# Bias copies, their source rows and the softmax statistics on GpSimd's DMA queue, with a smaller descriptor scratch

## The chip, the cores and the metric

One core of one Trainium2 chip runs the whole program. The metric is device time of one launch in microseconds (us); less is better. PE is TensorE, DVE VectorE, ACT ScalarE, POOL GpSimd and SP SyncE. SP computes nothing here: it only issues transfers. Every engine works through its own list of instructions in a fixed order, and a waiting instruction holds back all that stands behind it on its engine.

## The reference

Two layers (DEPTH) over 512 tokens of width 1024, batch 1. Each layer norms the residual, projects it once, and feeds four attention branches:

```python
for l in range(DEPTH):
    xn = rms_norm(x, norm_gain[l])
    (A: q k v z iq ik iw), (B: q k v z), (C: q kv pe z), (D: q k v z), gates = combined_projection(xn, w_in[l])
    ya = dsa_attention(...)                  # A: each query keeps its 128 best keys; bias per head and distance
    yb = dilated_mixture(qbm, kbm, b_v, rel_bias)   # B: 3 groups, steps 1, 4, 16
    yc = causal_dense_attention(qc, kc, v)   # C: latent attention with a rotary key
    yd = banded_attention(qd, kd, d_v, D_WINDOW - 1, band_bias(bias_d, 1), sinks[l])   # D
    merged = sum(sigmoid(gates[n]) * ((ys[n] * silu(zs[n])) @ w_branch[l, n]) for n in range(4))
    x = x + merged @ w_out[l]
```

Three things in it matter here. The bias of a score depends only on the distance of query and key: `rel_bias[t5_bucket(distance)]`, a row of numbers per head, shifted by one for each next query. The table `rel_bias` is one for both layers. And B joins its three groups by weights from the softmax maximum and denominator of each:

```python
m_all = jnp.stack(ms)
w = jnp.stack(dens) * jnp.exp(m_all - jnp.max(m_all, axis=0, keepdims=True))
w = w / jnp.sum(w, axis=0, keepdims=True)
return sum(w[g][..., None] * outs[g] for g in range(3))
```

## The kernel before

Products are taken exactly enough in three passes over weights split into a high and a low part: banks of 128 tokens x 384 columns (lines 512 to 514) or of 128 features x 512 tokens (lines 536 to 538). The weights come as a stream of slots. For each slot `next_slot` (397) issues one load on SP (402, tile `cbuf<-wall` in the trace) into a ring of four buffers; ACT makes the high part (405), DVE, and now and then POOL, the low part (411), into a ring of six. A load waits until the buffer that it overwrites has been read.

`plan` gives the order of a layer's jobs: the indexer, branch D (two slots groups, d0 and d1), the input of C, branch C, branch B (four pairs of heads, each with its groups 0, 1, 2 and then a `mix`), branch A, the merges, the output. A scheduler then reorders the instructions of each engine by a simulated timeline, and gives tiles their place in on-chip memory by itself, up to the memory's end.

The bias takes four steps. A one-hot product (335) makes the row of every head, in four chunks of 480 columns; DVE copies a chunk to a tile `th` (337) and a transfer writes it to `gdram` in HBM (338). `make_skew` (340) then has a transfer copy two rows, 128 times each, from HBM to HBM (347; one row for C, whose bias is a mask). There are 21 such copies: 4 for D, 1 for C, 12 for B, 4 for A, all in layer 1; both layers load from them. `load_bias` (365) last loads a tile from a copy with a row pitch one less than the copy's width, so that row i comes out shifted by i (372). `next_skew` takes copies from a list in the order D, C, B, A and puts them behind the weights requested so far by `tc.issue_after`, which orders instructions on SP.

After D's projections, POOL scales the normed queries and keys (660, 776), computes the norms (378, 379, 792, 793), starts the transfers that swap halves of a key tile (701, 702, `U<-U`) and later multiplies probabilities by one over their sum (958), before they are transposed for the product with V.

In B's groups 1 and 2 the tokens stand in another order (by residue class). Their statistics tile `st` therefore goes to HBM (`sd`, 1183) and comes back in token order (`nat`, 1185); the second transfer waits until the first has landed. The `mix` starts with `mn` on DVE (1111, 1112), which waits for `nat`.

Of the kernel before, what the change touches and what calls it, by code (L numbers as in the profile page):

```python
# [22 lines left out]
NT = S // 128  # L23
# [59 lines left out]
def job_slots(job):  # L83
    """Per weight slot: a list of (source, rows of 128, columns)."""
    kind = job[0]
    if kind in ("idx", "cin", "pair", "d0", "d1"):
        c = chunk_cols(job)
        return [[("w_in", 2 * i + j, c) for j in range(2)] for i in range(4)]
    if kind == "z":
        c = Z_OFF[job[1]] + job[2] * 128 + np.arange(128)  # L90
        return [[("w_in", 4 * i + j, c) for j in range(4)] for i in range(2)]
    if kind == "merge":
        n, ft = job[1], job[2]
        c = OFF_G + n * D + ft * 128 + np.arange(128)
        f = ft * 128 + np.arange(128)
        return [[("w_in", j, c) for j in range(6)],
                [("w_in", j, c) for j in (6, 7)] + [(("w_branch", n), j, f) for j in range(4)]]
    if kind == "out":
        f = job[1] * 128 + np.arange(128)
        return [[("w_out", 4 * i + j, f) for j in range(4)] for i in range(2)]  # L100
    if kind == "cq":
        q = job[1] * 384 + np.arange(384)
        return [[("w_q_b", 0, q), ("w_q_b", 1, q)]]
    if kind == "ckv":
        p = job[1]
        h = np.arange(64)
        kv = np.concatenate([(2 * p) * 128 + h, (2 * p + 1) * 128 + h,
                             (2 * p) * 128 + 64 + h, (2 * p + 1) * 128 + 64 + h])
        return [[("w_kv_b", 0, kv)]]
    raise ValueError(kind)  # L110


def plan():
    """The order of a layer's work; what comes first is preferred where several pieces are ready."""
    w = [("idx",)]
# [126 lines left out]
def build(ctx, tc, A, depth=2, dump=None):  # L242
# [46 lines left out]

# [1 line left out]
    def m_tiles():  # L291
# [26 lines left out]
    def later_consts():  # L318
        sy.dma_start(rope, A["rope"])
        sf = T([128, 512], F32, "ssq")[:, :384][:38].rearrange("p (g c) -> p g c", g=3)  # L320
        sy.dma_start(sf, A["sel"])
        ve.tensor_copy(sel, sf)
        rb = T([128, 256], F32, "qn")[:33, :C_ROW + 1]
        sy.dma_start(rb, A["relb"])
        rhl = T([128, 1024], F32R, "qk")[:33, :2 * (C_ROW + 1)].rearrange("p (e c) -> p e c", e=2)
        ve.tensor_copy(rhl[:, 0], rb)
        ve.tensor_tensor(rhl[:, 1], rb, rhl[:, 0], op=OP.subtract)
        for i in range(4):
            oh = T([128, 512], F32, "tmp")[:33, :480]
            sy.dma_start(oh, A["onehot"][:, i * 480:(i + 1) * 480])  # L330
            ohr = T([128, 1024], F32R, "qk")[:33, :480]
            ac.copy(ohr, oh)
            o = ps_t()
            for e in range(2):
                mm(o[:C_ROW + 1, :480], rhl[:, e], ohr, start=e == 0, stop=e == 1)
            gs = T([128, 512], F32, "th")[:C_ROW + 1, :480]
            ve.tensor_copy(gs, o[:C_ROW + 1, :480])
            sy.dma_start(gdram[:, i * 480:(i + 1) * 480], gs)

    def make_skew(seg, r):  # L340
        """Rows r and r + 1 of a segment, 128 copies each, so that a load can shift copy i by i."""
        r0, nr = (C_ROW, 1) if seg == "C" else (SEG_ROWS[seg][0] + r, 2)
# [3 lines left out]
        g = gdram[r0:r0 + nr, o:o + w]  # L346
        sy.dma_start(d, bass.AP(tensor=g.tensor, offset=g.offset, ap=[[SEG_LEN, nr], [0, 128], [1, w]]))
        for i in range(nr):
# [10 lines left out]
    def next_skew():  # L359
        """The next segment's copies, behind the weights requested so far."""  # L360
        if skews:
# [3 lines left out]
    def load_bias(row, seg, n):  # L365
        """[128, n] tile whose row i is the segment's row shifted by i to the right."""
        while (seg, row) not in skew:
# [7 lines left out]
    def rsqrt(eng, r, ss, n, scale, eps=EPS):  # L375
        """r = 1 / sqrt(ss * scale + eps) on [128, n]."""
        y = T([128, 8], F32, "nx")[:, :n]
# [4 lines left out]
    def layer(l, xt):  # L382
# [1 line left out]
        lay = cbuf[:, 520:1440]  # L384
# [7 lines left out]
        sy.dma_start(pk, A["pk"][l][:, :PK])  # L392
# [1 line left out]
        wpos, lcnt = [0], [0.0]  # L394
# [18 lines left out]

# [1 line left out]
        def gain_parts():  # L415
            """x * gain as hi and lo per row tile: the first products need not wait for the norm."""
            xg = [T([128, 2, 512], F32R, "y") for _ in range(4)]
# [56 lines left out]

# [1 line left out]
        pn = ps_t()  # L476
# [40 lines left out]
        def t_banks(slots, w, x):  # L517
            """Banks of all token tiles, filled together; x: hi and lo per row tile."""
            os = [ps_acc() for _ in range(NT)]
# [11 lines left out]
        def f_bank(parts, mh, ml, w=S):  # L531
            """parts: (hi, lo) stationary views [128, 128] per row tile; moving operands mh, ml: [128, w] each."""
            o = ps_acc()
# [10 lines left out]
        def split_ps(hi, lo, src, scale=None):  # L544
            """hi + lo = src (* scale), src in PSUM."""
            if scale is None:
# [10 lines left out]

# [1 line left out]
        def do_idx():  # L559
# [76 lines left out]

# [1 line left out]
        def evac(o, n, scale=1.0):  # L638
            """A copy of a bank's first n columns, so that the bank is free before the norms are known."""
            raw = T([128, 512], F32, "raw")[:, :n]  # L640
# [6 lines left out]
        def norm_qk(o, t, x, gi, scale=1.0):  # L647
            """o: two heads of q and of k in PSUM; hi and lo of the normed ones to x[:, t], [128, 4, 2, 64]."""
            o = evac(o, 256, scale)
# [19 lines left out]
        def q_out(uq, qx, hf, h0, n, perm):  # L669
            """Heads of qx [128, 2, n, 2, 64] (half hf of the tokens) to uq[:, h0:h0 + n], feature-major."""  # L670
            for i0 in range(0, n, 2):
# [12 lines left out]
        def k_out(kk, x, hf, perm):  # L684
            """The two k heads of x (half hf of the tokens), hi on top of lo, to kk(h, 0)."""
            p = ps_t(F32R)
# [11 lines left out]
        def k_swap(kk):  # L698
            """kk(h, 1): lo on top of hi."""
            for h in range(2):  # L700
# [82 lines left out]
        def do_cin():  # L783
# [21 lines left out]
            for i, c in enumerate((R_CQ, R_CQS)):  # L805
                ve.tensor_tensor(rtab[:, i], rope[:, i], pk[:, None, c:c + 32].to_broadcast([128, NT, 32]), op=OP.mult)
            # rotary key, shared by the heads
            t1 = T([128, 256], F32, "qn")[:, :128][:, :NT * 32].rearrange("p (t d) -> p t d", t=NT)
# [23 lines left out]
        def do_cq(p, cT):  # L832
            """The normed and rotated queries of two pairs, [128, 2, 4, 96] per half of the tokens."""
            h, lo = next_slot(("cq", p))
# [64 lines left out]

# [1 line left out]
        STEPS = {  # L901
# [5 lines left out]
        def scores(kind, step, qk, bias, nm, den, mask, sink, both):  # L907
            """exp of the scores less their maximum, sums to den, minus the maximum to nm."""
            s = ps_s()
# [51 lines left out]
        def attend(kind, qk, v, bias, nm, den, norm, both, mask=None, sink=None):  # L961
            """qk(qb, k0, n): (lhsT, rhs) of the passes; v(kb): stationary [128, 128]; nm/den [128, NT] columns.
            Returns the O bank: rows of V's high part on top of rows of its low part."""
            o = ph = pl = None
# [72 lines left out]
        def o_sum(dst, o, h, perm):  # L1037
            """Add the halves of an O bank into rows h*64.. of dst, in token order."""
            a, b = (0, 64) if h == 0 else (64, 0)
# [102 lines left out]

# [1 line left out]
        ys = [[None] * 4 for _ in range(4)]  # L1144
# [3 lines left out]
        for w in PLAN:  # L1148
# [20 lines left out]
            elif kind == "attB":  # L1169
# [11 lines left out]
                if g:  # L1181
                    sd = T([128, 16], F32, "sd", dp)
                    sy.dma_start(sd, stt_[:, g].rearrange("p t a h -> p (t a h)"))
                    sv = sd.rearrange("p (t e) -> (p t) e", e=4).rearrange("(t j) e -> j t e", j=128)
                    sy.dma_start(nat[:, g].rearrange("p t a h -> p t (a h)"), sv)
            elif kind == "mix":
# [142 lines left out]
```

## Time and profile before

| | us |
|---|---|
| median of 3 runs | 1953.87 (1952.23 to 1957.49) |
| profiled execution, span | 1949.2 |
| PE busy in it | 1884.5 (97%) |
| DVE busy | 1331.1 (68%) |
| ACT busy | 1103.0 (57%) |
| POOL busy | 728.5 (37%) |

For the profiled execution no time of its own is given beside its span; the median of the runs is 4.7 us above the span. Matmuls are pipelined, so PE's 97% says that PE rarely stands, not that it does its work at the highest rate: the granted clock has to be looked at as well, and where PE does stand it is asked what ended the wait. Waits of the other engines cost nothing unless PE waits for them in turn. A letter q behind an engine's name (SPq, POOLq) is its instruction queue, where transfers are issued.

### The profile page before, as it was taken

How to read it: one execution, taken by the hardware profiler on the slowest of the kernel's cores; microseconds unless marked ns; L12 is line 12 of the kernel's file. 1: busy time of each engine (PE TensorE's matmuls, PEld its weight loads, DVE VectorE, ACT ScalarE, POOL GpSimd, SP SyncE). 2: the span in 40 equal slices, each digit the busy share in tenths (PEclk: the TensorE clock that was granted, in tenths of full speed). 3: DMA queues.
4: the chain of work that ended last, by engine and by line, in shares of the span. 5: the costliest groups of instructions: out<-in, count | busy, mean ns of one | idle time of the engine just before them, and what ended most of it. 6: DMA issues, size and time to landing. Idle time of an engine off the chain costs nothing.

```text
span 1949.2 us, 33221 instructions
## 1 busy us (share of the span) xinstructions
PE 1884.5 (97%) x11348; PEld 1695.6 (87%) x11348; DVE 1331.1 (68%) x3410; ACT 1103.0 (57%) x2650; POOL 728.5 (37%) x1186
## 2 busy tenths in 40 slices
PE   8759999999989999999999999999999999999999
PEld 7648889989878998998889988899899989898887
DVE  7649777758476866665469888676768686766542
ACT  6538666656455565554347776566555656555431
POOL 3615353424233346640005345253343343755000
PEclk9879999999989999999999999999999999999999
DMA  4223233342334243332252222233333333333233
GB/s 163 84 91 95 67 90 103 105 113 88 110 105 118 80 121 105 99 98 82 91 187 85 82 66 93 74 88 83 94 105 113 101 101 91 117 96 101 80 92 108
DMA packets 103420, 193.47 MB, mean 99 GB/s; under 512 B 21510, under 2 KB 35924, under 8 KB 103252
## 3 DMA queue, kind: packets, MB, share of 16 engines
q1 hardware_dynamic: 92372, 173.52, 29.4%
q0 software_dynamic: 10880, 17.83, 4.2%
q8 instruction: 90, 1.47, 0.3%
q14 instruction: 78, 0.64, 0.1%
HBM read 168.84 MB, written 12.83 MB: 93 GB/s over the span
## 4 chain that ended last, share of the span: by engine, by line
PE 88%; DMA 4%; DVE 2%; ACT 2%; POOL 2%; issue 1%; SPq 1%; DVEq 0%; ACTq 0%; POOLq 0%
PE acc L537 14%; PE acc L536 14%; PE acc L538 14%; PE acc L512 9%; PE acc L513 9%; PE acc L514 9%; PE S L923 4%; PE T L994 3%; PE T L1014 2%; DMA cbuf<-wall 1%; DMA sd<-st 1%; PE T L1033 1%; PE T L1026 1%; PE T L676 1%; PE T L689 1%
## 5 line engine op out<-in xcount | busy, mean ns | idle before, releaser
L411 DVE TENSOR_TENSOR cbufr<-cbuf,cbufr 128x768 fp32r<-128x768 f32 (+3 forms) x396 | 357.6, 906 | 140.5 <-ACT cbufr L405 139.0
L405 ACT CAST cbufr<-cbuf 128x768 fp32r<-128x768 f32 (+3 forms) x396 | 304.9, 774 | 262.4 <-PE acc L537 195.9
L513 PE MATMUL acc<-cbufr 128*128 128x384 f32 (+1 forms) x1152 | 365.8, 318 | 0.0
L512 PE MATMUL acc<-cbufr 128*128 128x384 f32 (+1 forms) x1152 | 364.1, 317 | 0.0
L514 PE MATMUL acc<-cbufr 128*128 128x384 f32 (+1 forms) x1152 | 363.9, 316 | 0.0
L536 PE MATMUL acc<-cbufr 128*128 128x512 f32 x896 | 354.5, 396 | 0.9 <-ACT raw L642 0.9
L538 PE MATMUL acc<-cbufr 128*128 128x512 f32 x896 | 353.9, 395 | 0.0
L537 PE MATMUL acc<-cbufr 128*128 128x512 f32 x896 | 353.6, 395 | 0.0
L513 PEld LDWEIGHTS acc<-cbufr 128*128 128x128 f32 x1152 | 218.7, 190 | 3.0 <-issue 1.1
L512 PEld LDWEIGHTS acc<-cbufr 128*128 128x128 f32 x1152 | 218.5, 190 | 2.7 <-ACT U L696 0.7
L514 PEld LDWEIGHTS acc<-cbufr 128*128 128x128 f32 x1152 | 218.7, 190 | 2.3 <-issue 0.8
L379 POOL TENSOR_TENSOR nr<-nx,cbuf 128x4 f32<-128x4 f32 (+2 forms) x200 | 211.6, 1060 | 11.1
L538 PEld LDWEIGHTS acc<-cbufr 128*128 128x128 f32 x896 | 168.9, 188 | 34.0
L536 PEld LDWEIGHTS acc<-cbufr 128*128 128x128 f32 x896 | 169.0, 189 | 32.7 <-ACT raw L642 1.3
L537 PEld LDWEIGHTS acc<-cbufr 128*128 128x128 f32 x896 | 169.1, 189 | 32.3 <-issue 0.7
L958 POOL TENSOR_SCALAR P<-P,rd 128x128 f32<-128x128 f32 x192 | 117.3, 621 | 195.4 <-DVE rd L956 136.2
L378 POOL TENSOR_SCALAR nx<-nss 128x4 f32<-128x4 f32 (+2 forms) x200 | 62.3, 311 | 272.2 <-DVE nss L653 243.1
L701 POOL DMA_DIRECT2D U<-U x68 | 39.3, 578 | 311.4 <-ACT U L693 190.4
L547 ACT CAST PT<-T 128x128 fp32r<-128x128 f32 (+2 forms) x224 | 102.9, 478 | 64.0 <-PE T L994 38.0
L548 DVE TENSOR_TENSOR PT<-T,PT 128x128 fp32r<-128x128 f32 (+2 forms) x224 | 119.8, 548 | 22.0 <-ACT PT L547 20.3
L945 ACT ACTIVATE P<-P,nm 128x128 f32<-128x128 f32 x192 | 101.9, 533 | 57.4 <-DVE nm L942 56.7
L642 ACT COPY raw<-acc 128x256 f32<-128x256 f32 (+2 forms) x192 | 70.4, 377 | 107.9 <-PE acc L514 74.9
(256 smaller groups left out, 3954.0 us busy)
## 6 DMA issues: line engine op xcount, KB each, us to landing
cbuf<-wall SPq DMA_DIRECT2D x284, 384.0 KB
cbuf<-wall SPq DMA_DIRECT2D x96, 256.0 KB
U<-U POOLq DMA_DIRECT2D x136, 128.0 KB, 2.8
bias<-skew SPq DMA_DIRECT2D x32, 128.0 KB
bias<-skew SPq DMA_DIRECT2D x16, 256.0 KB
skew<-gdram SPq DMA_DIRECT2D x8, 384.0 KB
cbuf<-wall SPq DMA_DIRECT2D x8, 328.0 KB
skew<-gdram SPq DMA_DIRECT2D x4, 640.0 KB
```

The lines of the kernel that those rows point to most:

```text
L379: gp.tensor_tensor(r, y, mhalf[:, :n], op=OP.pow)
L405: pin(ac.copy(h, raw))
L411: pin(e.tensor_tensor(lo, raw, h, op=OP.subtract))
L512: mm(o[:, :c1 - c0], x[kt][:, 0, ts], h[:, a + c0:a + c1], start=kt == 0, stop=False)
L513: mm(o[:, :c1 - c0], x[kt][:, 0, ts], lo[:, a + c0:a + c1], start=False, stop=False)
L514: mm(o[:, :c1 - c0], x[kt][:, 1, ts], h[:, a + c0:a + c1], start=False, stop=kt == KT - 1)
L536: mm(o[:, :w], h, mh[kt], start=kt == 0, stop=False)
L537: mm(o[:, :w], h, ml[kt], start=False, stop=False)
L538: mm(o[:, :w], lo, mh[kt], start=False, stop=kt == n - 1)
L547: ac.copy(hi, src)
L548: ve.tensor_tensor(lo, src, hi, op=OP.subtract)
L958: gp.tensor_scalar(p[:, off:off + nk * 128], p[:, off:off + nk * 128], rd[:, qb:qb + 1], 0.0, op0=OP.mult, op1=OP.add)
```

## The change

Four calls move from SP (`sy`) to GpSimd (`gp`): the write of the bias rows (338), the copies (347), the statistics' way out (1183) and their way back (1185). The loads of weights (402) and of shifted bias tiles (372) stay on SP. The scratch in which descriptors of GpSimd's transfers are kept becomes 4096 bytes per partition instead of the default 16384; tiles may then lie in the 12 KB that become free. All else in the diff is comments.

```diff
@@ later_consts
             ve.tensor_copy(gs, o[:C_ROW + 1, :480])
-            sy.dma_start(gdram[:, i * 480:(i + 1) * 480], gs)
+            gp.dma_start(gdram[:, i * 480:(i + 1) * 480], gs)
@@ make_skew
         g = gdram[r0:r0 + nr, o:o + w]
-        sy.dma_start(d, bass.AP(tensor=g.tensor, offset=g.offset, ap=[[SEG_LEN, nr], [0, 128], [1, w]]))
+        gp.dma_start(d, bass.AP(tensor=g.tensor, offset=g.offset, ap=[[SEG_LEN, nr], [0, 128], [1, w]]))
@@ layer, attention of B
                     sd = T([128, 16], F32, "sd", dp)
-                    sy.dma_start(sd, stt_[:, g].rearrange("p t a h -> p (t a h)"))
+                    gp.dma_start(sd, stt_[:, g].rearrange("p t a h -> p (t a h)"))
                     sv = sd.rearrange("p (t e) -> (p t) e", e=4).rearrange("(t j) e -> j t e", j=128)
-                    sy.dma_start(nat[:, g].rearrange("p t a h -> p t (a h)"), sv)
+                    gp.dma_start(nat[:, g].rearrange("p t a h -> p t (a h)"), sv)
@@ module
-    nc = bacc.Bacc("TRN2", target_bir_lowering=False, num_devices=1)
+    nc = bacc.Bacc("TRN2", target_bir_lowering=False, num_devices=1, dynamic_dma_scratch_size=4096)
```

SP's list, from the last one-hot loads in layer 1 on, before: `gdram<-th` are the four chunks, `skew...` and `skewC` the copies.

```order
L330 DMA tmp_590<-onehot 33x480
L402 DMA cbuf<-wall 128x512
L338 DMA gdram<-th_567 41x480
L338 DMA gdram<-th_577 41x480
L347 DMA skewC_1298<-gdram 128x1x640
L402 DMA cbuf<-wall 128x512
L338 DMA gdram<-th_587 41x480
L402 DMA cbuf<-wall 128x512
L347 DMA skew_0_600<-gdram 256x1x384
L338 DMA gdram<-th_597 41x480
L347 DMA skew_2_602<-gdram 256x1x384
L347 DMA skew_4_1051<-gdram 256x1x384
```

The same place on SP now:

```order
L330 DMA tmp_590<-onehot 33x480
L402 DMA cbuf<-wall 128x512 x4
L372 DMA bias_1301<-skew_0_600 128x256
L372 DMA bias_1366<-skew_0_600 128x256
L372 DMA bias_1473<-skew_2_602 128x256
L402 DMA cbuf<-wall 128x512 x2
L402 DMA cbuf<-wall 128x768
```

Between two of SP's weight loads there is now nothing but loads of bias tiles. On POOL in the same stretch, now (`qk` is the tile of normed queries and keys, `U` a key tile):

```order
L338 DMA gdram<-th_567 41x480
L338 DMA gdram<-th_577 41x480
L378 TENSOR_SCALAR nx_971<-nss_968 128x6
L616 AFFINE_SELECT cbuf<-cbuf 128x128
L379 TENSOR_TENSOR nr_970<-nx_971,cbuf 128x6
L347 DMA skewC_1298<-gdram 128x1x640
L347 DMA skew_0_6521<-gdram 256x1x640
L347 DMA skew_2_6827<-gdram 256x1x640
L347 DMA skew_4_7172<-gdram 256x1x640
L347 DMA skew_6_7583<-gdram 256x1x640
L660 TENSOR_SCALAR qk_608<-qn_644 128x4x64
```

The four copies for A, the largest and the last to be used, come ahead of those for D, since the chunks that they read are written first. Further down POOL's list, ahead of the first multiplication of D's probabilities, now:

```order
L347 DMA skew_2_4372<-gdram 256x1x256
L701 DMA U_142_605<-U_142_605 64x512
L702 DMA U_142_605<-U_142_605 64x512
...
L347 DMA skew_4_4717<-gdram 256x1x384
L347 DMA skew_4_5127<-gdram 256x1x256
L347 DMA skew_4_5269<-gdram 256x1x256
L347 DMA skew_6_5623<-gdram 256x1x384
L347 DMA skew_6_5968<-gdram 256x1x256
L347 DMA skew_6_6379<-gdram 256x1x256
L379 TENSOR_TENSOR nr_1141<-nx_1142,cbuf 128x2
...
L958 TENSOR_SCALAR P_1310<-P_1310,rd_1318 128x128
```

All 21 copies now stand on POOL ahead of D's attention, where before eight stood on SP up to there and thirteen later, between the weights of C and B. A transfer of GpSimd waits in addition, by the semaphores that it is given in turn, until the transfer eight before it on GpSimd has landed. In B the two transfers of the statistics follow one another on POOL:

```order
L660 TENSOR_SCALAR qk_4579<-qn_4658 128x4x64
L1183 DMA sd_4460<-st_3976 128x16
L1185 DMA nat_3977<-sd_4460 128x4x4
L701 DMA U_1056_4476<-U_1056_4476 64x512
```

Before, SP had a load of weights between the two; now POOL itself waits between them until `sd` has landed, and the swap of the next key tile stands behind. In all, SP has 361 rows in its list before and 282 now, POOL 1175 and 1232.

## Rows read from the trace of the kernel before

**Rows 1.** Waits of PE in the whole span: total, times, longest us.
```profile
PE T L803 <- DVE PT L796: 22.3, 1, 22.3
PE T L1026 <- DVE PT L548: 12.3, 3, 5.2
PE T L676 <- ACT raw L642: 11.7, 1, 11.7
```

**Rows 2.** Chain of waits, 60 to 140 us: start, us, what.
```profile
81.64 14.50 DMA gdram<-th
...
113.80 7.30 SPq L347
...
121.62 13.52 DMA cbuf<-wall
```

**Rows 3.** Busy time by stretch: PE, PEld, DVE, ACT, POOL, PEclk, DMA share, GB/s.
```profile
86.00:96.00 10.00, 0.00 (x0) 0.00 (x0) 0.00 (x0) 0.00 (x0) 0.00 (x0) 0.57 0.13 50
...
122.00:135.00 13.00, 0.00 (x0) 0.00 (x0) 0.00 (x0) 0.00 (x0) 0.00 (x0) 0.50 0.25 85
```

**Rows 4.** Waits of all engines, 40 to 200 us.
```profile
POOL P L958 <- DVE rd L956: 34.3, 6, 26.6
...
ACT raw L642 <- DMA gdram<-th: 15.4, 1, 15.4
```

**Rows 5.** Lines 478, 1015 us apart: count, ns min/median/max, first and last start.
```profile
L478 PE MATMUL T<-cbuf,s x8: 251/251/272, 25.1 to 25.9; 128*128 128x2 f32 x8
...
L478 PE MATMUL T<-cbuf,s x8: 167/251/251, 1015.6 to 1016.3; 128*128 128x2 f32 x8
```

**Rows 6.** Chain of waits, first C heads and first two mixes of each layer.
```profile
199.69 0.77 PE T L895 x7
...
437.11 0.89 PE S L1135 x3
...
554.16 0.89 PE S L1135 x3
...
1154.73 0.77 PE T L895 x7
...
1388.72 0.89 PE S L1135 x3
...
1488.52 0.89 PE S L1135 x3
```

**Rows 7.** Chain of waits, 376 to 545 us, statistics of layer 1.
```profile
384.24 7.49 DMA sd<-st
...
528.75 10.47 DMA sd<-st
```

**Rows 8.** Waits of SP's queue, whole span; then SP's timeline in layer 2.
```profile
SPq L1185 <- DMA sd<-st: 46.5, 16, 9.8
...
1338.70 0.33 SPq L1183 DMA_DIRECT2D sd<-st  x1
...
1341.65 0.38 SPq L1185 DMA_DIRECT2D nat<-sd  x1
```

**Rows 9.** Lines 347 and 701: ns min/median/max, first and last start.
```profile
L347 SPq DMA_DIRECT2D skew<-gdram x20: 587/595/9925, 80.9 to 571.6; - x20
...
L701 POOL DMA_DIRECT2D U<-U x68: 514/584/754, 80.6 to 1799.3; - x68
```

**Rows 10.** Transfers of the whole span: line's tiles, times issued, KB of each.
```profile
skew<-gdram SPq DMA_DIRECT2D x8, 384.0 KB
...
skew<-gdram SPq DMA_DIRECT2D x4, 640.0 KB
skew<-gdram SPq DMA_DIRECT2D x8, 256.0 KB
```

**Rows 11.** POOL's timeline, 62 to 145 us and 376 to 402 us.
```profile
142.77 0.83 POOL L958 TENSOR_SCALAR P<-P,rd 128x128 f32<-128x128 f32 x2 [26.60 <-DVE rd L956]
...
399.88 0.63 POOL L701 DMA_DIRECT2D U<-U  x1 [19.74 <-ACT U L693]
```

## The prediction

> **What bounds the kernel now.** I read the waits of PE first, since PE is busy for 97% of the span and only its own idle time, or a lower rate, can be given back. Three waits carry nearly all of it: 22.3 us at line 803, 11.7 us at line 676, and 12.3 us in three pieces at line 1026 [rows 1]. The named releasers (DVE, ACT) are short instructions, so I asked what these had waited for. In the chain of waits between 60 and 140 us stand transfers and SP's queue: the last chunk of bias rows takes 14.50 us to land, SP stands 7.30 us in a copy of line 347, and then a weight slot takes 13.52 us [rows 2]. ACT waits 15.4 us for that chunk before it may write `raw`, which is what PE wants at line 676 [rows 4]. POOL waits 26.6 us just then, for DVE, so it is not the late one [rows 4, 11].
>
> What makes them late is seen in the busy time by stretch. From 86 to 96 us no engine computes anything, and the DMA share is 0.13, 50 GB/s: two engines of sixteen (2/16 = 0.125) [rows 3]. Only a copy is in flight there. A copy has two rows on its slowest dimension, and a 384 KB copy at 50 GB/s takes some 7.7 us; SP's 7.30 us in one is the same time. So before the change the copies go one behind the other on the same two engines, and SP waits with them; a weight slot or chunk, which needs all of its parts, waits behind them too. From 122 to 135 us PE is idle again, with a weight under way [rows 2, 3]. These idle stretches also have a granted clock of 0.57 and 0.50, near or at the 1.2 GHz level in place of 2.4 GHz.
>
> How much could come back is measured by layer 2, which does the same work without copies. From line 478 to the first C heads (line 895) layer 1 takes 199.69 - 25.1 = 174.6 us, layer 2 1154.73 - 1015.6 = 139.1 us [rows 5, 6]: 35.5 us. Of these 22.3 + 11.7 = 34.0 us are PE's two waits; the rest I leave to the bias product, which layer 1 alone has. From line 895 to the second mix layer 1 takes 354.5 us and layer 2 333.8 us [rows 6]: 20.7 us, of which 17.3 lie between the first and the second mix (117.1 against 99.8). There `sd` takes 7.49 and 10.47 us to land, against 1341.65 - 1338.70 = 2.9 us in layer 2 [rows 7, 8], and PE has its 12.3 us at line 1026. The copies run on until 571.6 us [rows 9]: thirteen of 21 come late, among B's weights. After the second mix both layers keep the same pace, so about 35 + 21 = 56 us is all that there is.
>
> **The change part by part.** *Copies leave SP.* Weights no longer stand behind copies in SP's queue. The wait at line 803 (22.3 us) goes whole: the slot of 13.52 us would land as others do. Of line 676's 11.7 us I leave 5: its chunk now follows five copies on POOL's queue, and if those are spread over other engines, it shares some with them for a part of the 14.50 us it takes today.
>
> *Copies come to POOL.* 21 copies and 4 chunks are 25 issues at about 0.58 us, the price of POOL's own transfers [rows 9]: 14.5 us. Between 70 and 115 us POOL is itself needed for scaling and norms; it also has gaps, 26.6 us of waiting before the first line 958 [rows 4, 11]. I take half as exposed, 7.5 us (bounds: 0 if the gaps take all of it, 14.5 if none). Behind the copies stand the swaps of `U` and the norms of C's input, and PE's scores and C's projections wait for these. That is the price if POOL only issues. If it must stand while a copy runs, as SP does, the price is another (first rival).
>
> *The thirteen late copies go early.* In B nothing then holds up `sd` or weights. Of 20.7 us I take 18 back; the rest is work that layer 1 may order differently (bounds 12.3, PE's named waits alone, and 20.7).
>
> *The statistics.* POOL waits between the two transfers for `sd`: 16 times 2.9 us = 46 us of standing, the sum that SP's queue has today (46.5 us [rows 8], with layer 1's slow ones in it). Behind it on POOL stand swaps of key tiles and norms of the next pair. POOL has gaps of the right kind, such as 19.74 us before the swap at 399.88 us [rows 11], and SP no longer stands there. I take 4 us, a quarter of a microsecond for each, between -5 (weights come earlier in B) and +46 (nothing hidden), nearer the low end since that gap is several times the standing.
>
> *Smaller scratch.* 12 KB per partition more for tiles: PE's waits name no buffer, so nothing. A ring a quarter the size may hold fewer descriptors: priced in the rival.
>
> Sum: -(34.0 - 5 - 7.5) - 18 + 4 = -35.5 us. The profiled span of 1949.2 becomes 1913.7, and with the 4.7 us by which the median stands above it, 1918 us. The terms' bounds give 1953.9 - 34.0 - 20.7 - 5 = 1894 at best. With 11.7 left at line 676, 14.5 of issue exposed and 12.3 back in B, the standing as taken, it is 1953.9 - 7.8 - 12.3 + 4 = 1938; the standing's own upper end of 46 would add 42 more and is left to the wide range. I take 1900 to 1938 as this case's own range.
>
> A rule of the Trainium skill speaks against the gain: transfers started by different engines end on the same 16 DMA engines and interleave, and starting from several engines saves only the time of starting them ("DMA: Bandwidth & Descriptors", Issuing engines are not separate DMA queues). In this trace starting is not small, 7.30 us for a copy [rows 2], so the rule and a gain can both hold; taken literally it would leave the copies' 50 GB/s as it is, which is the first rival. Another section of that page (Why a DMA increments its semaphore by 16 and not by 1) says that a GpSimd transfer of few parts takes consecutive engines from a cursor that moves on, where SP's takes the lowest ones always. The two engines of rows 3 fit SP's half; no run here yet shows GpSimd's. By it eight copies in flight would use all 16 engines, and the forecast holds.
>
> **The rivals.** *First: the copies still run one at a time and POOL stands for them.* The 21 copies are 8 x 384 + 4 x 640 + 8 x 256 + 320 = 8000 KB [rows 10], the 320 being that of C in the lists of the change. At 384 KB in 7.3 us that is 152 us. All stand on POOL ahead of the first line 958. They can start at about 72 us, so line 958 would start at about 224 instead of 142.8 us [rows 11]: 81 us late. PE's list holds D's transposes behind that and the early waits are swallowed; the late part still gives 18 back. 1953.9 + 81 - 18 + 4 = 2021 us. For it: the copies' form, two parts, is unchanged; SP stood for copies just so; the scratch is cut to a quarter; the four largest copies, for A, now run first. Against: POOL's transfers so far took 0.51 to 0.75 us each, two or four together, without standing [rows 9]. It decides once about one copy is in flight at a time; at one and a half, the delay is 152/1.5 - 71 = 30 us, and the sum is still slower. Range 1960 to 2060.
>
> *Second: two to three copies in flight, gains and delays nearly cancel.* With two, the copies end at 72 + 76 = 148 us: line 958 is some 5 us late and the early 21.5 us do not come; late part and statistics as above: 1953.9 + 5 - 18 + 4 = 1945. With more POOL standing in B (16 times 1 us in place of a quarter) 1957. So 1936 to 1960. For it: a POOL transfer waits for the landing of the one eight before, so the queue is not free either; and a share of the chunk lands behind copies as today.
>
> *Third: it doesn't do what it says*, because line 803 or B's pace hangs on something else, such as the ring of weight buffers. Against it stands layer 2, which has the same rings and no such waits. It would leave 1950 to 1958, a chance of 0.03.
>
> **How the numbers follow.** The forecast has 0.55, the first rival 0.28, the second 0.14, the third 0.03. This kernel's runs tell 0.3%, about 6 us, from no change. Faster, below 1948: all of the forecast (0.54) and somewhat under half of the second (0.06), 0.60. Within 0.3%, 1948 to 1960: 0.05 of the second, 0.01 of the forecast and 0.02 of the third, 0.08. Slower: 0.28 and 0.04, 0.32. The range for 8 in 10 goes from 1899 to 2020: a tenth is left above it, half of the first rival, and a few hundredths below. Likeliest: 1918 us.
>
> **What would show it.** If right: SP's timeline from 64 to 140 us has no issue of 7 us or more; no stretch with a DMA share of 0.13 and idle engines; PE's waits at lines 803 and 676 are gone or small; a copy's issue on POOL lasts under 1 us; the first line 958 starts at 105 to 125 us; `sd` lands in about 3 us in both layers; the first to the second mix takes about 100 us in layer 1. Layer 2 keeps its pace within a few us. The first rival shows as issues of line 347 of 5 us and more on POOL and a line 958 after 190 us. If line 958 is early and the mixes are late, the statistics' term was mis-sized; if line 803 still waits for a weight, the copies hold the engines and not the queue.

## The result and the profile after

The changed kernel takes 2084.98 us (median of 4 runs, 2083.68 to 2086.16) against 1953.14 us for the kernel before: a ratio of 1.0668, 95% interval 1.0653 to 1.0683, 132 us slower. The forecast was 1918 us, and the range up to 2020 us did not hold the time either. The likeliest case was wrong in sign. The first rival, that GpSimd stands for one copy at a time, is what the trace shows, at a higher price than it was given.

The profiled execution has a span of 2084.4 us, 135.2 us above that of before. First the waits of PE after the change (total, times, longest, in us), to be held against [rows 1]:

```profile
PE T L676 <- DVE qk L777: 80.0, 1, 80.0
PE T L676 <- DVE qk L661: 40.9, 1, 40.9
PE T L803 <- DVE PT L796: 40.1, 1, 40.1
PE S L923 <- DMA U<-U: 9.4, 1, 9.4
```

Four waits make 170.4 us, where 35.3 us stood at the same places before (22.3, 11.7 and, at line 923, 1.3). The wait in B at line 1026 has gone from 12.3 to 1.8 us, so what was hoped for in B did come. DVE, the named releaser, is again only a link: its `qk` at lines 661 and 777 needs the two products of POOL at lines 660 and 776, and its `PT` at line 796 needs POOL's norm `nr` of line 379. DVE's own waits from 60 to 300 us show it:

```profile
DVE PT L796 <- POOL nr L379: 93.0, 2, 48.0
...
DVE qk L777 <- POOL qk L776: 44.7, 3, 37.4
...
DVE qk L661 <- POOL qk L660: 44.1, 1, 44.1
```

POOL's timeline says why its products are late (start, us, engine, line, operation, count, idle time before and what ended it):

```profile
71.88 1.10 POOL L347 DMA_DIRECT2D skew<-gdram  x1
88.72 1.08 POOL L347 DMA_DIRECT2D skew<-gdram  x1 [15.74 <-issue]
104.37 1.05 POOL L347 DMA_DIRECT2D skew<-gdram  x1 [14.57 <-issue]
119.91 1.06 POOL L347 DMA_DIRECT2D skew<-gdram  x1 [14.48 <-issue]
120.99 0.79 POOL L660 TENSOR_SCALAR qk<-qn 128x256 fp32r<-128x256 f32 x2
...
223.90 0.57 POOL L776 TENSOR_SCALAR qk<-qn 128x128 fp32r<-128x128 f32 x2
...
290.73 1.06 POOL L347 DMA_DIRECT2D skew<-gdram  x1 [7.48 <-issue]
291.81 0.72 POOL L379 TENSOR_TENSOR nr<-nx,cbuf 128x2 f32<-128x2 f32 x1
...
293.44 0.83 POOL L958 TENSOR_SCALAR P<-P,rd 128x128 f32<-128x128 f32 x2
```

The first of A's copies goes out at once. Each of the next three waits 14 to 16 us, for no semaphore that the profile shows ("issue"), and the scaling at line 660, which stood at 69.99 us before, starts at 120.99 us. The last copy is issued at 290.73 us, and the first line 958 follows at 293.44 us, against 142.77 us [rows 11]. How long POOL stands, and how long a copy takes, is in line 347's own view and in the page's list of transfers (times issued, KB, us to landing):

```profile
L347 POOL DMA_DIRECT2D skew<-gdram x20: 1054/1063/1154, 71.9 to 290.7; - x20
...
issue: 176.4, 19
```

```profile
skew<-gdram POOLq DMA_DIRECT2D x8, 384.0 KB, 10.7
...
skew<-gdram POOLq DMA_DIRECT2D x4, 640.0 KB, 15.3
skew<-gdram POOLq DMA_DIRECT2D x8, 256.0 KB, 8.4
skewC<-gdram POOLq DMA_DIRECT2D x1, 320.0 KB, 4.4
```

Ahead of the last copy nineteen others of two rows have to land: 8 x 10.7 + 4 x 15.3 + 7 x 8.4 = 205.6 us. From 71.88 to 290.73 us are 218.9, 7.4 of them spent waiting for the last chunk. So these copies go one at a time, the next issued when the one before has landed; only C's, which has one row, goes out beside A's first, at 71.24 us. In between lie long stretches in which no engine computes (POOL's 1.15 us are two issues; busy time by stretch; PE, PEld, DVE, ACT, POOL, granted clock, DMA share, GB/s), and the share of the DMA engines is again that of two of sixteen, as in [rows 3]:

```profile
95.00:120.00 25.00, 0.00 (x0) 0.00 (x0) 0.00 (x0) 0.00 (x0) 1.15 (x2) 0.50 0.13 44
```

The rest of the account comes from the same two markers as in the prediction, line 895 and layer 2's line 478; first before, then after (count, ns, first and last start):

```profile
L895 PE MATMUL T<-cbuf,cq x64: 270/273/279, 197.8 to 1262.0; 128*96 128x128 f32 x64
```

```profile
L895 PE MATMUL T<-cbuf,cq x64: 270/273/280, 348.3 to 1395.6; 128*96 128x128 f32 x64
...
L478 PE MATMUL T<-cbuf,s x8: 167/251/252, 1149.5 to 1150.2; 128*128 128x2 f32 x8
```

Up to line 895 the loss is 348.3 - 197.8 = 150.5 us, which is the delay of line 958 (150.7). From there to layer 2 the stretch shrinks from 1015.6 - 197.8 = 817.8 to 801.2 us: 16.6 us come back. Layer 2 to the end takes 934.9 us against 933.6. 150.5 - 16.6 + 1.3 = 135.2 us.

### The profile page after: what moved, and what is told of

The parts are those of the page before. It is cut to its first block, busy times and chain, and to the rows that moved or that the text cites. A ratio compares the mean times of both kernels' runs of the same rounds, so it can differ in the third digit from the quotient of the medians.

```text
span 2084.4 us, 33192 instructions
## 1 busy us (share of the span) xinstructions
PE 1888.2 (91%) x11348; PEld 1696.3 (81%) x11348; DVE 1334.1 (64%) x3410; ACT 1104.0 (53%) x2650; POOL 757.3 (36%) x1243
## 5 line engine op out<-in xcount | busy, mean ns | idle before, releaser
L958 POOL TENSOR_SCALAR P<-P,rd 128x128 f32<-128x128 f32 x192 | 112.5, 597 | 185.4 <-DVE rd L956 111.5
L676 PE MATMUL T<-cbufr,qk 128*128 128x128 f32 x320 | 44.1, 249 | 120.9 <-DVE qk L777 80.0
L676 PEld LDWEIGHTS T<-cbufr,qk 128*128 128x128 f32 x320 | 35.4, 143 | 123.9 <-DVE qk L777 80.4
## 6 DMA issues: line engine op xcount, KB each, us to landing
skew<-gdram POOLq DMA_DIRECT2D x8, 384.0 KB, 10.7
skew<-gdram POOLq DMA_DIRECT2D x4, 640.0 KB, 15.3
```

The lines of the kernel that those rows point to most:

```text
L958: gp.tensor_scalar(p[:, off:off + nk * 128], p[:, off:off + nk * 128], rd[:, qb:qb + 1], 0.0, op0=OP.mult, op1=OP.add)
```

## The experiments

Theory R says that the descriptor scratch is the limit: a copy gives 128 parts to each of only two DMA engines, and 4096 bytes have room for one such copy. Its rivals are S, that copies of GpSimd's queue are serial by nature, and E, that the two DMA engines are the limit whatever is in flight. All kernels below are cut from the two kernels by a line or two; times are medians, ratios are to the kernel before on the same chip.

**Twice the scratch.**

```diff
-dynamic_dma_scratch_size=4096
+dynamic_dma_scratch_size=8192
```

> The changed kernel with a descriptor scratch of 8192 bytes in place of 4096; nothing else. Theory R (room): the changed kernel's copies go one at a time because each gives 128 parts to each of two DMA engines, and the scratch of 4096 has room for the parts of one copy beside those of small transfers, not of two. With twice the scratch at least two, perhaps three, are in flight: GpSimd's 176 us of standing before line 347 fall to 50 to 90 us, the first line 958 starts at 145 to 185 us instead of 293, and the time is 1940 to 1985 us. Theory S (serial): copies of GpSimd's queue run one behind the other whatever the scratch: the standing stays near 176 us and the time within 10 us of 2085. Theory E (engines): more are in flight, but on the same two DMA engines: GpSimd stands less before the first ones, but all copies together still take some 200 us, and the time stays above 2040.

Measured: 1957.02 us, ratio 1.0021 (1.0011 to 1.0031). 128 us of the 132 are gone with this number alone. POOL's timeline now shows three copies leaving together and the fourth waiting:

```profile
70.20 3.22 POOL L347 DMA_DIRECT2D skew<-gdram  x3
88.24 1.07 POOL L347 DMA_DIRECT2D skew<-gdram  x1 [14.82 <-issue]
...
105.99 3.30 POOL L347 DMA_DIRECT2D skew<-gdram  x3 [7.52 <-DMA gdram<-th]
```

```profile
L347 POOL DMA_DIRECT2D skew<-gdram x20: 1054/1066/1154, 70.2 to 163.6; - x20
...
issue: 50.5, 11
```

The standing falls from 176.4 to 50.5 us and the copies are issued by 163.6 us. S is out. So is E: a 384 KB copy still lands in a median of 12.1 us with up to three in flight, against 10.7 alone, so the copies in flight were not sharing two engines. Even so the kernel is no faster than before, since PE still waits for POOL's products, 10.8 us by way of line 661 and 25.9 by way of line 777:

```profile
PE T L676 <- DVE qk L777: 25.9, 1, 25.9
```

The change with the default scratch of 16384 bytes was not run.

**Half as many parts in each transfer.**

```diff
-        gp.dma_start(d, bass.AP(..., ap=[[SEG_LEN, nr], [0, 128], [1, w]]))
+        for c in (0, 64):
+            gp.dma_start(d[:, c:c + 64], bass.AP(..., ap=[[SEG_LEN, nr], [0, 64], [1, w]]))
```

> The changed kernel with each copy made by two transfers of 64 repeats: same bytes, same scratch, same two engines for each transfer, 64 parts on each instead of 128. Theory R (room): three halves fit where one whole did, one and a half times as much is in flight: 220 us of copying become about 147, the first line 958 starts near 220 us, time 1990 to 2040 us. If one transfer at a time were the rule, whatever its size: 2080 to 2100.

Measured: 1965.80 us (two runs, 1965.29 and 1966.32), ratio 1.0069 (1.0051 to 1.0088); better than expected. Line numbers are one higher in it.

```profile
70.46 2.45 POOL L348 DMA_DIRECT2D skew<-gdram  x3
82.06 0.81 POOL L348 DMA_DIRECT2D skew<-gdram  x1 [9.15 <-issue]
```

With 4096 bytes, three halves leave together and the fourth waits, just as three whole copies did with 8192. That is room counted in parts: 3 x 64 on an engine fit and 4 x 64 don't; 1 x 128 fits and 2 x 128 don't; with 8192, 3 x 128 fit and 4 x 128 don't. It is not counted in bytes moved: at 4096 one copy of 640 KB fits, but two of 256 KB don't; where one follows another in the changed kernel, it waits 7.5 to 7.7 us. The size of the gain was missed because I scaled the 220 us by 1.5; the copies are all issued by 186 us, 116 us after the first, since half of a 384 KB copy lands in 8.1 us and three halves are in flight.

**The same copies over 16 engines, still on GpSimd.**

```diff
-        gp.dma_start(d, bass.AP(..., ap=[[SEG_LEN, nr], [0, 128], [1, w]]))
+        gp.dma_start(d.rearrange("r c w -> c r w"), bass.AP(..., ap=[[0, 128], [SEG_LEN, nr], [1, w]]))
```

> The changed kernel with the 128 repeats as the slowest dimension of a copy instead of the two rows: same bytes, same order, 16 DMA engines instead of two, 16 parts for each. Theories R and E: no standing before line 347 beyond a few us, copies land in 2 to 4 us, first line 958 at 100 to 120 us, time 1905 to 1925 us. Theory S: a shorter copy stands less too, 21 times 3 to 4 us, first line 958 near 150 us, time 1940 to 1955.

Measured: 1923.37 us, ratio 0.9849 (0.9835 to 0.9864). The standing is gone, as R says: with 4096 bytes four of these copies leave together, each of as many parts as before in all, but with 16 on an engine. So it is the parts on one engine that count, not those of the whole copy. The kernel is faster than before, but the first line 958 comes at 127.7 us and not by 120. What is late now (busy time by stretch, then waits between 60 and 150 us, the last of them SP's from 60 to 140):

```profile
100.00:110.00 10.00, 0.51 (x3) 0.08 (x1) 0.00 (x0) 0.00 (x0) 4.84 (x13) 0.64 1.01 286
110.00:120.00 10.00, 5.51 (x14) 4.40 (x15) 5.73 (x17) 3.28 (x6) 5.79 (x9) 0.51 1.00 285
```

```profile
ACT cbufr L405 <- DMA cbuf<-wall: 23.2, 4, 19.3
DVE cbufr L411 <- ACT cbufr L405: 17.8, 3, 17.2
...
PE T L676 <- DVE qk L777: 14.0, 1, 14.0
```

```profile
SPq L372 <- DMA skew<-gdram: 23.8, 2, 23.1
```

ACT waits 19.3 us for a weight slot, DVE for ACT, and PE for the `qk` that stands behind this on DVE. Two things make the weight late. SP stands 23.1 us, until 95.8 us, at the load of a bias tile (line 372) that waits for its copy, and the weights stand behind it. And all 21 copies go out between 70 and 114 us, so that the DMA engines are full: 256 KB loads of weights from 99 to 116 us land in 10.5 us, where the median of the whole run is 2.7. Another queue for the copies spares the weights neither.

**Only the copies back on SP.**

```diff
-        gp.dma_start(d, bass.AP(...))
+        sy.dma_start(d, bass.AP(...))
```

> The changed kernel with line 347 alone back on SP; chunks and statistics stay on GpSimd, scratch 4096. All theories: the loss of 131 us is the copies' alone, so the time is near that of before: 1940 to 1965 us. The first line 958 near 143 us. If the statistics' standing on GpSimd were worth what its upper bound said (46 us), it would be 1985 to 2000.

Measured: 1943.21 us, ratio 0.9950 (0.9935 to 0.9965). The loss is the copies' alone; chunks and statistics on GpSimd gained 10 us beside copies on SP. PE's wait at line 803 stays (28.1 us), that at line 676 goes.

**Only the smaller scratch.**

```diff
-bacc.Bacc("TRN2", target_bir_lowering=False, num_devices=1)
+bacc.Bacc("TRN2", target_bir_lowering=False, num_devices=1, dynamic_dma_scratch_size=4096)
```

> The kernel before with a descriptor scratch of 4096 bytes, nothing else. Theory R: only the swaps U<-U use it, and they are small: same, 1948 to 1959 us. If the smaller scratch by itself cost something (waits of GpSimd before line 701) or gave something through tiles' places, the time would differ by over 6 us and GpSimd's wait before line 701 would have changed.

Measured: 1953.29 us, ratio 0.9998 (0.9989 to 1.0008): nothing. The smaller scratch costs only together with transfers that fill it.

**Only the statistics on GpSimd, beside the kernel before.**

```diff
-                    sy.dma_start(sd, ...)
+                    gp.dma_start(sd, ...)
-                    sy.dma_start(nat[:, g]..., sv)
+                    gp.dma_start(nat[:, g]..., sv)
```

> The kernel before with lines 1183 and 1185 alone on GpSimd; copies and chunks stay on SP, scratch as before. It splits the 10 us that the version with only the copies back on SP was below before. Theory A (the statistics): sd lands in about 3 us, no load of weights stands behind nat's wait on SP, the wait at line 1026 goes from 12.3 to under 6 us, time 1941 to 1948 us. Theory B (the chunks, whose landing fell from 14.5 to 3.5 us, and the wait at line 676): 1950 to 1957 us.

Measured: 1946.82 us, ratio 0.9969 (0.9958 to 0.9980). This is theory A: PE's wait at line 1026 falls from 12.3 to 3.4 us, while line 803 keeps 21.9; `sd` lands in 6.0 us at most, against the 10.47 of [rows 7]. It is 6 of the 10 us above. That the other 4 are the chunks' is a subtraction; chunks alone on GpSimd beside copies on two engines were not run.

**Only the statistics back on SP, in the changed kernel** (the edit before, the other way).

> The changed kernel with the statistics back on SP; copies and chunks on GpSimd, scratch 4096. It prices the statistics' step where no late copies run beside it. By the versions with spread copies, moving them to GpSimd costs 5 us there, so this is 2076 to 2083 us. If the step gains 6 us, as it did beside the kernel before, it is 2088 to 2094.

Measured: 2082.42 us, ratio 1.0667 (1.0652 to 1.0681), against 1.0668 for the changed kernel: no difference that can be told. The time lies at the upper edge of the first range, but each of the two expectations was a difference, and the ratios show none. The stretch from line 895 to layer 2 is 801.0 us here and 801.2 there.

**Spread copies on SP, with and without the rest of the change.** The edit is the spreading shown above, with `sy` in place of `gp`: first on the kernel before and nothing else.

> The kernel before with the copies on SP as before, but the 128 repeats as their slowest dimension, so that 16 DMA engines share each; nothing of the change. If the early loss of before (35.5 us) is the copies' time on two engines, waits at lines 803 and 676 shrink to under 10 us together and the time is 1905 to 1925 us. If it is SP's standing for anything in front of the weights, whatever its shape, or the copies' bytes, the time stays above 1940 us.

Measured: 1899.13 us, ratio 0.9727 (0.9714 to 0.9740), 54 us faster than before without a single transfer moved to another queue, and 6 us below the range expected. PE's largest waits and line 347:

```profile
PE acc L526 <- ACT cbufr L405: 6.0, 1, 6.0
PE T L676 <- ACT raw L642: 4.6, 1, 4.6
```

```profile
L347 SPq DMA_DIRECT2D skew<-gdram x20: 536/542/1217, 80.4 to 519.0; - x20
```

The wait at line 803 no longer exists, line 676 keeps 4.6 us, and no issue of a copy lasts over 1.2 us, where 9.9 us were the longest [rows 9]. Then with chunks and statistics on GpSimd and the small scratch as well:

> The changed kernel (chunks and statistics on GpSimd, scratch 4096) with the copies on SP, spread over 16 engines. Against the spread copies on GpSimd (1923 us), where all 21 went between 70 and 114 us and filled all engines while the weights waited 19 us, SP sends them between the weights. If that bunching is what was left there, this is 1900 to 1915 us, with no wait of PE over 8 us after the start. If bunching cost nothing, 1918 to 1928.

Measured: 1904.55 us, ratio 0.9754 (0.9740 to 0.9768); and with the statistics alone on GpSimd:

> The version with spread copies on SP and only the statistics on GpSimd; chunks on SP, scratch 16384. If the chunks' queue no longer matters once copies are short, within 5 us of the version with chunks on GpSimd too; if a chunk on SP still holds up the weights, 5 to 15 us above it.

Measured: 1904.42 us, ratio 0.9759 (0.9746 to 0.9772). Sending the copies between the weights instead of all at once is worth 19 us against the spread copies on GpSimd. But both versions are 5 us above the one that leaves the statistics on SP. Between the two, the queue of the chunks and the scratch make no difference.

**The fastest: spread copies on SP, chunks alone on GpSimd.**

```diff
-            sy.dma_start(gdram[:, i * 480:(i + 1) * 480], gs)
+            gp.dma_start(gdram[:, i * 480:(i + 1) * 480], gs)
```

> The kernel before with spread copies on SP (1899 us) and the chunks of line 338 alone on GpSimd; statistics stay on SP, scratch 16384. The two versions with statistics on GpSimd were 5 us above the one without, and chunks on GpSimd brought line 895 forward from 164.6 to 159.7 us. If both hold by themselves, it is 1891 to 1897 us and the fastest. If the statistics' 5 us were a reordering that any such move brings, 1897 to 1906.

Measured: 1891.34 us, ratio 0.9686 (0.9672 to 0.9699). PE's waits, and line 895:

```profile
PE acc L526 <- ACT cbufr L405: 6.6, 1, 6.6
PE T L1026 <- DVE PT L548: 1.4, 2, 1.0
```

```profile
L895 PE MATMUL T<-cbuf,cq x64: 270/273/279, 158.5 to 1203.7; 128*96 128x128 f32 x64
```

Only the wait for the first weights is left. Line 895 comes 39 us earlier than before, 3.8 us more than the 35.5 us by which layer 2 was quicker there. So with the statistics on SP the chunks' move is worth 8 us, and with the statistics on GpSimd nothing; why was not followed.

## Why the prediction was wrong

**What bounds the kernel before: right, and now shown in the main.** The copies sit on two of sixteen engines, and weights and chunks are late because of them. Spreading the same copies gave 54 us, and with the chunks 62, which is more than the 56 us that were said to be all there is. Whether the weights were late by SP's standing or by the shared engines is not separated: spreading the copies ended both.

**Copies come to POOL: the step that failed.** It charged 7.5 us of issue, "the price if POOL only issues". POOL did not only issue: it stood 176.4 us, and line 895 came 150.5 us later. The evidence that I leaned on, GpSimd's swaps going out two or four together, was of transfers too small to fill the scratch; it said nothing of transfers with 128 parts on an engine. The chances were set the wrong way round between the forecast and the first rival.

**Copies leave SP: only half true.** The weights no longer stand behind the copies, but they stand behind the bias loads of line 372, which stayed on SP and wait for the copies. D's first copy goes out fifth, at 137.55 us, and until 148.30 us SP stands for it (SP's waits, 60 to 300 us):

```profile
SPq L372 <- DMA skew<-gdram: 85.3, 3, 74.8
```

From 73.5 to 159.8 us no load of weights is issued. POOL's products come later still, so PE's waits end with POOL; what SP's standing would cost by itself is not shown in this kernel. With the copies spread on GpSimd, 23.1 us of it stood ahead of PE's wait of 14.0 us.

**Smaller scratch: right by itself, wrong in company.** "Nothing" holds for the scratch alone (0.9998). With the copies on the same queue it is the cause: doubling it takes away 128 us. The rival named it, as one of four reasons, and gave it no weight of its own.

**The first rival's size.** It took SP's 7.3 us for 384 KB and so 152 us of copying; on GpSimd's queue such a copy takes 10.7 us from issue to landing, and the copying lasts 220. Of the 64 us by which the rival's 2021 us were short of 2085, these 68 are all. The delay itself went through one to one, as the rival said: line 958, and with it line 895, came 150 us late. Its sign, issues of 5 us and more, did not come: an issue lasts 1.05 to 1.15 us, and the standing is the idle time before it. Why a copy takes longer is visible in part. With one 640 KB copy in flight, from 88.8 to 104.3 us after the change, and with copies alone in flight from 86 to 96 us before, the rate in forty slices of the stretch and the DMA packets were:

```profile
GB/s 0 0 0 0 17 17 57 57 55 53 53 53 53 40 53 53 53 53 53 53 53 53 53 53 53 53 53 53 53 53 53 66 53 53 53 53 53 26 0 0
DMA packets 1040, 0.66 MB, mean 43 GB/s; under 512 B 912, under 2 KB 912, under 8 KB 1040
```

```profile
GB/s 49 49 49 49 57 43 49 41 51 49 49 49 49 49 49 49 49 49 55 49 55 49 49 49 49 49 46 55 48 48 61 48 48 55 48 48 55 48 46 49
DMA packets 317, 0.50 MB, mean 50 GB/s; under 512 B 9, under 2 KB 301, under 8 KB 317
```

While it moves, the copy on GpSimd's queue is not the slower one: 53 GB/s in most slices, against 49. But nothing moves in its first four slices and its last two, 2.3 us together, where SP's copies follow one another without a gap. Twenty times 2.3 us would be 46 of the 68, by estimate, and 7.4 more are the wait for the last chunk; the rest stays open. On GpSimd's queue 912 of 1040 packets are under 512 B, on SP's 9 of 317; why was not settled, and the rates do not show a price for it.

**Early waits.** The prediction took line 803's 22.3 us as gone and left 5 at line 676. They grew to 40.1 and 120.9 us, since POOL's scaling, its norms and the swaps stood behind the copies in POOL's order; the prediction had named just these as what is queued there.

**Late copies go early: right.** 18 us were taken back, and 16.6 came between line 895 and layer 2.

**Statistics: right in size here, but not of one sign.** +4 us was the term; in the changed kernel the step measures nothing (1.0668 against 1.0667). Beside slow copies on SP it gains 6 us, since `sd` and `nat` then leave the queue that they share with the copies. Beside spread copies it costs 5 us, and 13 between the fastest version and that with the statistics moved too and the small scratch. In the latter POOL stands 29.2 us at line 1185 for `sd`; by which way the loss then reaches PE was not followed further.

**Which engines the copies use.** With all copies on GpSimd and spread, the DMA share is 1.01, and weights from SP's queue need 10.5 us to land instead of 2.7. The Trainium skill says it so: transfers from all engines share the same 16 DMA engines ("DMA: Bandwidth & Descriptors", Issuing engines are not separate DMA queues). It also says there that the time to start a transfer is usually small beside the transfer; that did not hold here, where POOL stood 14 to 16 us ahead of 640 KB copies that land in 15.3. With 8192 bytes of scratch, copies of which three are in flight land in 12.1 us instead of 10.7. This agrees with the cursor of the Trainium skill by which GpSimd's transfers of few parts move on over the engines ("DMA: Bandwidth & Descriptors", Why a DMA increments its semaphore by 16 and not by 1). With room for one copy only, it gains nothing here.

## What to carry to other kernels

Before moving a transfer to another queue, ask how many DMA engines its shape uses and how many parts each of them gets: here the slowest dimension of two was most of the trouble, and swapping two dimensions on the old queue, for 54 us, was worth more than any move tried here. Don't give a queue whose issuer also computes transfers that it has to stand for; the price is not the transfer but all that waits in that engine's order behind it. Ask too what on the old queue still waits for the transfer that has left it. And small transfers that pass freely are no evidence for large ones: look for the resource that they fill.

## What the runs showed of the hardware

A transfer of GpSimd's that finds no room in the descriptor scratch does not fail; the engine stands, up to 15.7 us for one copy, and the profile calls it "issue", with no releaser named. Room goes by parts per DMA engine: at 4096 bytes one copy with 128 parts on each engine or three with 64, at 8192 three with 128. DRAM-to-DRAM copies on two engines moved at about 50 GB/s from either queue; one at a time from GpSimd's, each spent some 2.3 us more in which nothing moved. And in the stretches where all stood, the granted clock was 0.50, the 1.2 GHz level, and work after them starts slow: after the wait of 80 us, lines 536 to 538 took 0.63 us for a product from 225 to 229 us, at a granted clock of 0.50, and 0.39 us from 230 us on, at 1.00.
